# Attention block of a two-layer hybrid network: score products from stacked query halves, paired rms factors, and the first two query products placed ahead of the values

## The chip, the core and the metric

The kernel runs as one program on one core of a Trainium2 chip. The metric is the device time of one execution in microseconds. Five engines work side by side, each through its own instructions in a fixed order: TensorE (PE, with its weight loads shown as PEld), VectorE (DVE), ScalarE (ACT), GpSimd (POOL) and SyncE (SP). An instruction waits on semaphores for what it needs, and whatever is behind it on the same engine waits with it.

## The reference

The network has two layers, each a mixer and a feed-forward block with a short convolution. Layer 0 mixes by a convolution and a recurrence, layer 1 by sliding-window attention with a sink. Only the attention is touched here. T is 512, the width 1024, with 16 query heads in 4 groups that share 4 key and value heads of 64:

```python
h = rms_norm(x, norm_g)
qkv = h @ w_qkv + b_qkv
q = partial_rope(rms_norm(q, q_norm_g), positions)   # 16 heads
k = partial_rope(rms_norm(k, k_norm_g), positions)   # 4 heads
# blocks of 128 queries against the block before and their own: 256 keys
s = einsum('bnqhgd,bnkhd->bnhgqk', q, kc) * HEAD_DIM ** -0.5
s = where(valid, s, -inf)
m = maximum(max(s), sink)
pr = exp(s - m);  pr = pr / (sum(pr) + exp(sink - m))
o = einsum('bnhgqk,bnkhd->bnqhgd', pr, vc)
return o @ w_o + b_o
```

## The kernel before

Everything is kept transposed: a tile has 128 features in its partitions and the 512 positions along it. A large product goes as three products of halves: each weight chunk and each activation is split into a high half in the type fp32r and a low half, the rest. `gemm` (L162 to L175) loads a chunk of weights by SP (`wraw`, two buffers), makes its high half on ACT (`whi`, L150) and its low half on DVE (`wlo`, L151), with three buffers each, and issues twelve 128x512 matmuls (L174) for each half chunk of a single output block. A cast to `whi` can only start when PE is through with the half chunk three before it.

`attention` makes, in this order of the source: the products of the four key heads (two tiles), the row factor `rstd` (L224), the keys' own rms factor and rotation (`kr`) and their copy into the tiles `kd`, which hold a key head twice, in partitions 0 to 63 and again in 64 to 127; the values `vt` (L876, matmuls with 128x256); and then the queries, two heads a tile, by `queries(j)` for j = 0 to 7. `queries` reads its product out of PSUM (`zt`, L890), squares it on ACT (L892), sums the squares per position by sixteen tiny matmuls (L897), makes the rms factor `rq` of the two heads by five small DVE and two small ACT instructions (L902 to L910), and rotates the query (`rope`: four POOL DMAs into `zr`, then L836 to L838).

`block(m, b)` does the 4 heads of group m for the 128 queries of block b: four score matmuls in full fp32 (L931) from the 64 partitions of one head, each two instructions on the chip; on DVE the mask, the factor and the minimum (L936); the exponential on ACT (L101); the normaliser (L941 to L946, DVE); transposes on PE (L950) that ACT copies out (`pT`, L952); the product with the values (L957); and its split into `oh`, `ol` (L183 on ACT, L184 on DVE). The scores take the three PSUM banks of ring "c", two for each block.

The loop runs m from 0 to 3 and b from 0 to 3 in each, with `queries(2m+2)` and `queries(2m+3)` in between; `queries(0)` and `queries(1)` stand ahead of it. Then comes the output product with `w_o` (L174 again, 192 matmuls, 36 of which need only the first three groups). The order of the instructions on each engine is not that of the source: a scheduler, working from its own estimates, writes one fixed order per engine, and the chip keeps to it.

Of the kernel before, what the change touches and what calls it, by code (L numbers as in the profile page):

```python
# [11 lines left out]
F32 = mybir.dt.float32  # L12
F32R = mybir.dt.float32r
I32 = mybir.dt.int32
AF = mybir.ActivationFunctionType
ALU = mybir.AluOpType
# [3 lines left out]
P = 128  # L20
T = 512
D = 1024
DC = D // P
NB = T // P
# [11 lines left out]
NH = 16  # L36
NKV = 4
HD = 64
# [7 lines left out]
T3 = 5  # L46
# [22 lines left out]
class Net:  # L69
# [734 lines left out]
    def attention(self):  # L804
        nc, tc, ap = self.nc, self.tc, self.ap
        V, S, G = nc.vector, nc.scalar, nc.gpsimd
        wq, wo = ap["w_qkv"], ap["w_o"]
# [4 lines left out]
        xh, xl = self.xg_tiles()  # L812
        for m in range(DC):
            self.xg_chunk(xh, xl, "attn_norm_g", 0, m)
        with ExitStack() as es:
            pool = lambda **k: es.enter_context(tc.tile_pool(**k))
            cst = pool(name="atb", bufs=1)
# [7 lines left out]
            def rope(dst, z, j=None):  # L825
                t = tq("rp")
# [14 lines left out]
            kd = [cst.tile([P, T], F32, name=f"kd{m}") for m in range(NKV)]  # L841
# [11 lines left out]
            for i in range(2):  # L853
# [9 lines left out]
                kr = tq("kr")  # L863
                rope(kr, t)
                for e in range(2):
                    for o in range(2):
                        G.dma_start(kd[2 * i + e][o * HD : (o + 1) * HD, :], kr[e * HD : (e + 1) * HD, :])
# [15 lines left out]

            qr = cst.tile([P, 8, T], F32, name="qr")
            rq = cst.tile([P, NB, NH], F32, name="rq")

            def queries(j):
                pq = self.gemm(wq, j, xh, xl, m=1, pss=[self.bank("a")])[0]
                t = tq("zt")
                V.tensor_tensor(out=t, in0=pq, in1=rstd, op=ALU.mult)  # L890
                sq = tq("zs")
                S.activation(out=sq, in_=t, func=AF.Square, bias=self.pc("attn_b_qkv", j))  # L892
                pss = self.bank("d")[:, 0:8].rearrange("p (b h) -> p b h", b=NB)

                for b in range(NB):
                    for i in range(0, P, 32):
                        nc.tensor.matmul(pss[i : i + 32, b, :], lhsT=sq[:, b * P + i : b * P + i + 32], rhs=self.bh, start=True, stop=True,  # L897
                                         tile_position=(0, i))
                S.activation(out=t, in_=t, func=AF.Identity, scale=self.pc("attn_q_norm_g"), bias=self.bg[:, j : j + 1])

                ms = tr.tile([P, NB, 2], F32, tag="ms", name="ms")
                V.tensor_scalar(out=ms, in0=pss, scalar1=1.0 / HD, scalar2=1e-6, op0=ALU.mult, op1=ALU.add)  # L902
                rope(qr[:, j, :], t, j)
                y0 = tr.tile([P, NB, 2], F32, tag="my", name="my")
                self.fn(out=y0, in_=ms, func=AF.Ln)
                self.fn(out=y0, in_=y0, func=AF.Exp, scale=-0.5)
                V.tensor_tensor(out=ms, in0=ms, in1=y0, op=ALU.mult)
                V.tensor_tensor(out=ms, in0=ms, in1=y0, op=ALU.mult)
                V.tensor_scalar(out=ms, in0=ms, scalar1=0.5 / 8, scalar2=-1.5 / 8, op0=ALU.mult, op1=ALU.add)
                V.tensor_tensor(out=rq[:, :, 2 * j : 2 * j + 2], in0=ms, in1=y0, op=ALU.mult)  # L910

            cst.tile([P, 112], F32, name="gap")
# [3 lines left out]
            def block(m, b):  # L916
# [10 lines left out]
                for hp in range(2):  # L927
                    for e in range(2):
                        h = 4 * m + 2 * hp + e
                        hs = slice(e * HD, (e + 1) * HD)  # L930
                        nc.tensor.matmul(pscs[e][:, hp, :nk], lhsT=qr[hs, h // 2, bs], rhs=kd[m][hs, k0 : k0 + nk], start=True, stop=True)  # L931
# [29 lines left out]
            queries(0)  # L961
            queries(1)
# [82 lines left out]
```

## Time and profile before

| | us |
|---|---|
| median of three runs | 1217.86 (1217.53 to 1218.5) |
| the profiled execution | 1216.95 |
| its span in the trace | 1215.2 |
| PE busy, of the span | 1194.8 (98%) |
| DVE busy | 723.4 (60%) |
| ACT busy | 554.3 (46%) |

The time around the span is 1.75 us. The attention lies between about 668 and 850 us. In this document the block phase is the stretch from the first L936 (719.70 us) to the end of the last L946 (812.04 us). In a timeline row the first number is the start and the second the duration; PE durations are modelled and overlap, so what a matmul costs is read from the distance of two starts. In the table of windows each engine has its busy time and the count of its instructions.

### The profile page before, as it was taken

To read this page: it belongs to the slowest core of one execution; us is meant where nothing else is said; L and a number is where in the kernel's file an instruction comes from. 1 tells how busy PE (TensorE), PEld (TensorE's weight loads), DVE (VectorE), ACT (ScalarE), POOL (GpSimd) and SP (SyncE) were. 2 spreads that over 40 slices of the span, in tenths; PEclk is the share of its full clock that TensorE was granted. 3 is DMA by queue.
4 is the path that set the end of the run, shared out by engine and by line. 5 is a ranking of instruction groups with operands and counts; after the bars stand their busy time and mean duration, and the time that the engine had idled before them with its cause. 6 is when DMAs were issued, how large, how long until landed. Compare 5 with 4: busy or idle time off the path is not lost.

```text
span 1215.2 us, 16956 instructions
## 1 busy us (share of the span) xinstructions
PE 1194.8 (98%) x6419; PEld 940.5 (77%) x6419; DVE 723.4 (60%) x1366; ACT 554.3 (46%) x1035; POOL 72.0 (6%) x209
## 2 busy tenths in 40 slices
PE   6999999999999999999999999999999999999998
PEld 5777866568788888888888866668888888888886
DVE  6787866477766555553333778875555555553332
ACT  6878332374534444342222567764543343442221
POOL 4101031000100000000000031100000000000000
PEclk9999998999999999999999999999999999999999
DMA  6144291023322223233333231112222223233331
GB/s 191 37 130 113 96 221 38 2 88 103 97 92 104 94 97 104 87 104 96 96 96 95 87 95 57 41 36 90 101 90 101 103 89 104 88 103 112 113 113 61
DMA packets 65088, 114.43 MB, mean 94 GB/s; under 512 B 15680, under 2 KB 17936, under 8 KB 65008
## 3 DMA queue, kind: packets, MB, share of 16 engines
q1 hardware_dynamic: 60048, 102.25, 26.3%
q0 software_dynamic: 4816, 10.89, 3.5%
q8 instruction: 50, 0.82, 0.3%
q14 instruction: 30, 0.25, 0.1%
q10 hardware_dynamic: 144, 0.23, 0.1%
HBM read 105.40 MB, written 4.26 MB: 90 GB/s over the span
## 4 chain that ended last, share of the span: by engine, by line
PE 94%; DVE 2%; ACT 2%; DMA 1%; issue 1%; SPq 0%; DVEq 0%
PE mm L174 68%; PE bank L174 11%; PE mm L633 2%; PE bank L931 2%; PE bank L957 1%; PE bank L950 1%; PE ps L411 1%; PE ps L543 1%; DMA xT<-in_xT_dram 1%; PE ps L562 1%; PE ps L556 1%; PE ps L570 0%; PE bank L359 0%; PE ps L549 0%; PE ps L520 0%
## 5 line engine op out<-in xcount | busy, mean ns | idle before, releaser
L151 DVE TENSOR_TENSOR wlo<-wraw,whi 128x512 fp32r<-128x512 f32 x364 | 250.8, 690 | 348.0 <-ACT whi L150 347.4
L150 ACT CAST whi<-wraw 128x512 fp32r<-128x512 f32 x364 | 224.9, 619 | 421.3 <-PE mm L174 378.4
L174 PE MATMUL mm<-xgh,whi 128*128 128x512 f32 x896 | 350.9, 392 | 9.8 <-ACT whi L150 8.3
L174 PE MATMUL mm<-xgh,wlo 128*128 128x512 f32 x896 | 351.0, 392 | 0.2 <-DVE wlo L151 0.2
L174 PE MATMUL mm<-xgl,whi 128*128 128x512 f32 x896 | 350.5, 391 | 0.0
L174 PEld LDWEIGHTS mm<-xgh,whi 128*128 128x128 f32 x896 | 168.6, 188 | 47.0 <-ACT whi L150 10.1
L174 PEld LDWEIGHTS mm<-xgh,wlo 128*128 128x128 f32 x896 | 168.5, 188 | 38.7 <-issue 2.4
L174 PEld LDWEIGHTS mm<-xgl,whi 128*128 128x128 f32 x896 | 168.7, 188 | 35.8 <-issue 1.2
L174 PE MATMUL mm<-hh,whi 128*128 128x512 f32 x352 | 136.9, 389 | 0.0
L174 PE MATMUL mm<-hl,whi 128*128 128x512 f32 x352 | 136.9, 389 | 0.0
L174 PE MATMUL mm<-hh,wlo 128*128 128x512 f32 x352 | 136.9, 389 | 0.0
L174 PEld LDWEIGHTS mm<-hh,wlo 128*128 128x128 f32 x352 | 66.1, 188 | 13.8
L174 PEld LDWEIGHTS mm<-hh,whi 128*128 128x128 f32 x352 | 66.1, 188 | 13.8
L174 PEld LDWEIGHTS mm<-hl,whi 128*128 128x128 f32 x352 | 66.1, 188 | 13.5
L720 DVE SCALAR_TENSOR_TENSOR t<-gp,col,t 128x512 f32<-128x512 f32 x88 | 63.5, 745 | 0.0
L717 ACT ACTIVATE t<-gp,col 128x512 f32<-128x512 f32 x44 | 35.7, 816 | 35.3 <-DVE gp L715 34.7
L183 ACT CAST hh<-t 128x512 fp32r<-128x512 f32 x44 | 27.2, 622 | 36.8 <-DVE t L723 36.5
L715 DVE TENSOR_TENSOR gp<-mm,rstd 128x512 f32<-128x512 f32 x44 | 30.3, 692 | 17.3 <-PE mm L174 17.2
L723 DVE TENSOR_TENSOR t<-t,mm 128x512 f32<-128x512 f32 x44 | 30.1, 687 | 17.0 <-PE mm L174 17.0
L101 ACT ACTIVATE t<-t 128x512 f32<-128x512 f32 x44 | 27.7, 630 | 20.4 <-DVE t L720 20.3
L714 POOL MEMSET gp<- 128x2 f32 x44 | 4.5, 104 | 507.7 <-DVE t L720 451.0
L936 DVE CUSTOM_DVE_ANT_0 pr<-bank,mask,nsnk 128x256 f32<-128x256 f32 (+1 forms) x64 | 31.4, 503 | 1.9 <-PE bank L931 1.9
(328 smaller groups left out, 1433.6 us busy)
## 6 DMA issues: line engine op xcount, KB each, us to landing
wraw<-in_w_up_dram SPq DMA_DIRECT2D x88, 512.0 KB, 3.5
wraw<-in_w_down_dram SPq DMA_DIRECT2D x40, 512.0 KB, 3.5
wraw<-in_w_in_dram SPq DMA_DIRECT2D x22, 512.0 KB, 3.6
wraw<-in_w_qkv_dram SPq DMA_DIRECT2D x12, 512.0 KB, 3.5
wraw<-in_w_out_dram SPq DMA_DIRECT2D x8, 512.0 KB, 3.5
wraw<-in_w_o_dram SPq DMA_DIRECT2D x8, 512.0 KB, 3.5
st<-cpad POOLq DMA_DIRECT2D x24, 135.0 KB, 4.4
xT<-in_xT_dram SPq DMA_DIRECT2D x4, 512.0 KB, 8.2
```

The costliest lines, as they stand in the source:

```text
L101: ins = self.nc.scalar.activation(**kw)
L150: nc.scalar.copy(hi, src)
L151: nc.vector.tensor_tensor(out=lo, in0=src, in1=hi.bitcast(F32), op=ALU.subtract)
L174: mm = lambda a, b, **kw: self.nc.tensor.matmul(ps, lhsT=a[:, i, k, :], rhs=b[:, kk, :], **kw)
L183: nc.scalar.copy(hi, src)
L633: nc.tensor.matmul(pc[b * 32 : b * 32 + 32, :], lhsT=dg[:, b, g, :], rhs=stk[b][:, 4 * g : 4 * g + T], start=g == 0, stop=g == 7, tile_pos ...
L715: V.tensor_tensor(out=gp[:, 2:], in0=pg[i], in1=rstd, op=ALU.mult)
L717: S.activation(out=t, in_=gp[:, 2:], func=AF.Identity, scale=self.pc("ffn_conv_w", (3 * l + 2) * FC + f), bias=self.pc("ffn_conv_b", l * F ...
L720: V.scalar_tensor_tensor(out=t, in0=gp[:, j : j + T], scalar=self.pc("ffn_conv_w", (3 * l + j) * FC + f), in1=t, op0=ALU.mult, op1=ALU.add)
L723: V.tensor_tensor(out=t, in0=t, in1=pu[i], op=ALU.mult)
L931: nc.tensor.matmul(pscs[e][:, hp, :nk], lhsT=qr[hs, h // 2, bs], rhs=kd[m][hs, k0 : k0 + nk], start=True, stop=True)
L936: V.tensor_tensor_reduce(out=pr_[:, i, :nk], in0=pscs[e][:, hp, :nk], in1=mask[:, 2 * P - nk :], op0=ALU.add, op1=ALU.min, scale=rq[:, b, ...
```

## The change

The keys are split once into high and low fp32r halves (`ks`), and `kd` keeps both halves of a head, each in both partition halves. Each query tile is split after its rotation into `qh` (ACT) and `ql` (DVE), and four SP DMAs of 128 KB put them into `qs`, where a head has its high half in 64 partitions and its low half in the other 64. A score is now two fp32r matmuls over all 128 partitions, one with the keys' high and one with their low half, always over 256 keys (before: 128 in block b = 0). The rms factors are made for two query tiles at once: their sums of squares share one PSUM bank, and the small instructions run once for both. `queries(0)` and `queries(1)` now stand ahead of the values. The rotation's scratch `rp` and the tile `qr` moved to the ring "t2", and `kr` too.

```diff
-            kd = [cst.tile([P, T], F32, name=f"kd{m}") for m in range(NKV)]
+            kd = [cst.tile([P, 2, T], F32R, name=f"kd{m}") for m in range(NKV)]
+            pair = lambda n: tr.tile([P, 2, 2, T], F32R, tag="qs", name=n, bufs=2)
+            ks = pair("ks")
...
-                kr = tq("kr")
+                kr = t2("kr")
                 rope(kr, t)
+                self.split(ks[:, i, 0, :], ks[:, i, 1, :], kr)
                 for e in range(2):
                     for o in range(2):
-                        G.dma_start(kd[2 * i + e][o * HD : (o + 1) * HD, :], kr[e * HD : (e + 1) * HD, :])
+                        G.dma_start(kd[2 * i + e][o * HD : (o + 1) * HD].bitcast(F32), ks[e * HD : (e + 1) * HD, i].bitcast(F32))
...
             def queries(j):
...
-                pss = self.bank("d")[:, 0:8].rearrange("p (b h) -> p b h", b=NB)
+                if j % 2 == 0:
+                    qs["ps"] = self.bank("d")[:, 0:16].rearrange("p (b i h) -> p b i h", b=NB, i=2)
+                pss = qs["ps"][:, :, j % 2]
...
-                rope(qr[:, j, :], t, j)
+                qr = t2("qr")
+                rope(qr, t, j)
+                if j % 2 == 0:
+                    qs[j // 2] = pair("qs")
+                q = [tr.tile([P, T], F32R, tag="t2", name=n, bufs=T3) for n in ("qh", "ql")]
+                self.split(q[0], q[1], qr)
+                for e in range(2):
+                    for d in range(2):
+                        nc.sync.dma_start(qs[j // 2][d * HD : (d + 1) * HD, j % 2, e, :].bitcast(F32), q[d ^ e][e * HD : (e + 1) * HD, :].bitcast(F32))
+                if j % 2:
+                    ms = tr.tile([P, NB, 4], F32, tag="ms", name="ms")
...
+            queries(0)
+            queries(1)
             vt = cst.tile([P, NB, KD], F32, name="vt")
...
                 for hp in range(2):
-                    for e in range(2):
-                        h = 4 * m + 2 * hp + e
-                        hs = slice(e * HD, (e + 1) * HD)
-                        nc.tensor.matmul(pscs[e][:, hp, :nk], lhsT=qr[hs, h // 2, bs], rhs=kd[m][hs, k0 : k0 + nk], start=True, stop=True)
+                    for j in range(2):
+                        for e in range(2):
+                            nc.tensor.matmul(pscs[e][:, hp, :], lhsT=qs[m][:, hp, e, bs], rhs=kd[m][:, j, k0 : k0 + 2 * P], start=j == 0, stop=j == 1)
...
-            queries(0)
-            queries(1)
             for m in range(NKV):
```

The lines shift: the score matmul L931 becomes L948, L936 becomes L953, the values' L876 becomes L923, the sums of squares L897 become L888, and the transposes L950 become L967.

The scheduler's order changes with it. On PE 73 of the 192 query matmuls stand ahead of the first score matmul before, and 102 now. The two places below are those where the block phase begins.

On DVE before, up to the first instruction of the first block (`pr_6121`); `zt_6079` belongs to the third query tile, `ms` and `rq` are the rms factor's small instructions:

```order
L151 TENSOR_TENSOR wlo_6220<-wraw_6201,whi_6219 128x512
L836 TENSOR_TENSOR rp_5955<-zr0_5582,sgs_3292 128x512
L838 TENSOR_TENSOR qr_5891<-qr_5891,rp_5955 128x512
L890 TENSOR_TENSOR zt_6079<-bank_6044,rstd_5661 128x512
L151 TENSOR_TENSOR wlo_6368<-wraw_6365,whi_6367 128x512
L836 TENSOR_TENSOR rp_6029<-zr1_5583,sgs_3292 128x512
L902 TENSOR_SCALAR ms_6101<-bank_6083 128x8
L838 TENSOR_TENSOR qr_5891<-qr_5891,rp_6029 128x512
L837 TENSOR_TENSOR qr_5891<-zt_6079,cos_3252 128x512
L907 TENSOR_TENSOR ms_6101<-ms_6101,my_6111 128x8
L936 ISA pr_6121,nm_6119<-bank_6122,mask_3300,nsnk_3298,rq_5892 128x128
```

On DVE now, up to the same instruction (`pr_6136`); `ql_5914` is the low half of the second query tile, `wlo_6588` the weights' second half of the sixth, and `zt_6093` the third query tile:

```order
L184 TENSOR_TENSOR ql_5914<-qr_5904,qh_5913 128x512
L904 TENSOR_SCALAR ms_6296<-bank_6097 128x16
L908 TENSOR_TENSOR ms_6296<-ms_6296,my_6298 128x16
L909 TENSOR_TENSOR ms_6296<-ms_6296,my_6298 128x16
L910 TENSOR_SCALAR ms_6296<-ms_6296 128x16
L911 TENSOR_TENSOR rq_5772<-ms_6296,my_6298 128x4x4
L151 TENSOR_TENSOR wlo_6588<-wraw_6569,whi_6587 128x512
L836 TENSOR_TENSOR rp_6116<-zr0_5582,sgs_3292 128x512
L837 TENSOR_TENSOR qr_6115<-zt_6093,cos_3252 128x512
L838 TENSOR_TENSOR qr_6115<-qr_6115,rp_6116 128x512
L953 ISA pr_6136,nm_6134<-bank_6137,mask_3300,nsnk_3298,rq_5772 128x128
```

The factors of the third and fourth query tiles, a low half of the sixth tile's weights and the whole rotation of the third tile have come ahead of the first block.

On ACT before, up to the first exponential:

```order
L899 ACTIVATE zt_6005<-zt_6005,bg_3312,col_86 128x512
L101 ACTIVATE my_6037<-ms_6027 128x8
L101 ACTIVATE my_6037<-my_6037 128x8
L150 CAST whi_6219<-wraw_6201 128x512
L150 CAST whi_6367<-wraw_6365 128x512
L892 ACTIVATE zs_6081<-zt_6079,col_86 128x512
L899 ACTIVATE zt_6079<-zt_6079,bg_3312,col_86 128x512
L101 ACTIVATE my_6111<-ms_6101 128x8
L101 ACTIVATE my_6111<-my_6111 128x8
L101 ACTIVATE pr_6121,dn_6120<-pr_6121,nm_6119 128x128
```

On ACT now, from the high half of the first query tile (`qh_5840`) to the first exponential; `whi_6422` belongs to the fifth query tile's weights, `whi_6571` and `whi_6587` to the sixth's, `whi_6751` to the seventh's:

```order
L150 CAST whi_6422<-wraw_6404 128x512
L183 CAST qh_5840<-qr_5830 128x512
L881 ACTIVATE zs_6095<-zt_6093,col_86 128x512
L890 ACTIVATE zt_6093<-zt_6093,bg_3312,col_86 128x512
L150 CAST whi_6571<-wraw_6569 128x512
L183 CAST qh_5913<-qr_5904 128x512
L881 ACTIVATE zs_6260<-zt_6258,col_86 128x512
L890 ACTIVATE zt_6258<-zt_6258,bg_3312,col_86 128x512
L150 CAST whi_6587<-wraw_6569 128x512
L150 CAST whi_6751<-wraw_6749 128x512
L183 CAST qh_6125<-qr_6115 128x512
L101 ACTIVATE pr_6136,dn_6135<-pr_6136,nm_6134 128x128 x2
```

The splits of the queries stand behind weight casts, and each of those waits for PE to be through with the half chunk three before it.

## Rows read from the trace of the kernel before

**Rows 1.** Page, busy time, share of the span, instructions.

```profile
PE 1194.8 (98%) x6419; PEld 940.5 (77%) x6419; DVE 723.4 (60%) x1366; ACT 554.3 (46%) x1035; POOL 72.0 (6%) x209
```

**Rows 2.** Windows: stretch, length, then PE, PEld, DVE, ACT, POOL busy (instructions), clock, DMA.

```profile
684.80:719.70 34.90, 34.54 (x296) 26.67 (x295) 25.52 (x51) 17.80 (x33) 9.98 (x20) 1.00 0.40 111
719.70:812.04 92.34, 91.37 (x632) 57.94 (x631) 78.37 (x316) 69.57 (x218) 10.35 (x21) 1.00 0.13 39
812.04:814.68 2.64, 2.40 (x19) 1.35 (x18) 1.12 (x3) 1.74 (x4) 0.00 (x0) 1.00 0.03 6
```

**Rows 3.** Waits of DVE in the block phase: total us, times, longest.

```profile
DVE ol L184 <- ACT oh L183: 4.9, 11, 0.8
DVE ms L902 <- PE bank L897: 2.2, 4, 0.7
DVE pr L936 <- PE bank L931: 1.9, 5, 0.4
DVE zt L890 <- PE bank L174: 1.7, 3, 0.8
DVE dn L943 <- ACT nm L101: 1.5, 3, 1.0
DVE nm L941 <- ACT pr L101: 1.2, 2, 0.8
```

**Rows 4.** Timeline of DVE: rstd, around the first L936, the last L946.

```profile
684.80 0.43 DVE L224 COPY rstd<-rms_y 128x512 f32<-128x512 f32 x1
...
704.52 0.68 DVE L151 TENSOR_TENSOR wlo<-wraw,whi 128x512 fp32r<-128x512 f32 x1
705.12 0.68 DVE L838 TENSOR_TENSOR kr<-kr,rp 128x512 f32<-128x512 f32 x1
...
719.70 0.41 DVE L936 CUSTOM_DVE_ANT_0 pr<-bank,mask,nsnk 128x128 f32<-128x128 f32 x1 [0.36 <-PE bank L931]
...
810.90 1.14 DVE L946 TENSOR_SCALAR pr<-pr,dn 128x256 f32<-128x256 f32 x4
```

**Rows 5.** Timeline of PE: values' matmuls, query matmuls, the first scores, the end.

```profile
681.22 0.28 PE L876 MATMUL mm<-wlo,xgh 128*128 128x256 f32 x1
681.34 0.28 PE L876 MATMUL mm<-whi,xgl 128*128 128x256 f32 x1
...
698.02 0.39 PE L174 MATMUL bank<-xgl,whi 128*128 128x512 f32 x1
698.25 0.40 PE L174 MATMUL bank<-xgh,wlo 128*128 128x512 f32 x1
...
715.49 0.92 PE L931 MATMUL bank<-kd,qr 64*128 64x128 f32 x6
...
814.68 0.50 PE L174 MATMUL bank<-oh,whi 128*128 128x512 f32 x1
```

**Rows 6.** Windows of the score line alone: stretch, length, PE and PEld busy, clock, DMA.

```profile
719.70:812.04 92.34, 25.11 (x118) 14.16 (x116) 1.00 0.13 39
```

**Rows 7.** Timeline of PE: two runs of score matmuls and the matmul after each.

```profile
745.43 1.13 PE L931 MATMUL bank<-kd,qr 64*128 64x256 f32 x4
746.48 0.50 PE L174 MATMUL bank<-xgl,whi 128*128 128x512 f32 x1
...
783.38 1.56 PE L931 MATMUL bank<-kd,qr 64*128 64x256 f32 x8
784.87 0.50 PE L174 MATMUL bank<-oh,whi 128*128 128x512 f32 x1
```

**Rows 8.** Groups by form, 668 to 848 us: busy us, mean ns, idle before.

```profile
L902 DVE TENSOR_SCALAR ms<-bank 128x8 f32<-128x8 f32 x8 | 1.3, 164 | 2.9 <-PE bank L897 2.9
L150 ACT CAST whi<-wraw 128x512 fp32r<-128x512 f32 x40 | 24.7, 617 | 29.7 <-PE bank L174 23.1 <-PE mm L174 4.2 <-PE mm L876 2.3
L101 ACT ACTIVATE my<-my 128x8 f32<-128x8 f32 x8 | 1.7, 208 | 0.2
```

**Rows 9.** Tile kd: its DMAs from SBUF to SBUF, 128 KB each.

```profile
DMA to landing us min/median/max: 2.2/2.8/5.3
```

More of the change, by code (lines that the diff above doesn't have):

```diff
@@ L825, in rope @@
             def rope(dst, z, j=None):
-                t = tq("rp")
+                t = t2("rp")
                 if j is None:
@@ L838, in rope @@
                 V.tensor_tensor(out=dst, in0=dst, in1=t, op=ALU.add)
-            kd = [cst.tile([P, T], F32, name=f"kd{m}") for m in range(NKV)]
+            cst.tile([P, 56], F32, name="gap0")
+            kd = [cst.tile([P, 2, T], F32R, name=f"kd{m}") for m in range(NKV)]
+            pair = lambda n: tr.tile([P, 2, 2, T], F32R, tag="qs", name=n, bufs=2)
+            ks = pair("ks")
             pk = self.gemm(wq, 8, xh, xl)
@@ new lines, in attention, with queries @@
+            qs = {}
+            rq = cst.tile([P, NB, NH], F32, name="rq")
+            def queries(j):
+                pq = self.gemm(wq, j, xh, xl, m=1, pss=[self.bank("a")])[0]
+                t = tq("zt")
+                V.tensor_tensor(out=t, in0=pq, in1=rstd, op=ALU.mult)
+                sq = tq("zs")
+                S.activation(out=sq, in_=t, func=AF.Square, bias=self.pc("attn_b_qkv", j))
+                if j % 2 == 0:
+                    qs["ps"] = self.bank("d")[:, 0:16].rearrange("p (b i h) -> p b i h", b=NB, i=2)
+                pss = qs["ps"][:, :, j % 2]
+                for b in range(NB):
+                    for i in range(0, P, 32):
+                        nc.tensor.matmul(pss[i : i + 32, b, :], lhsT=sq[:, b * P + i : b * P + i + 32], rhs=self.bh, start=True, stop=True,
+                                         tile_position=(0, i))
+                S.activation(out=t, in_=t, func=AF.Identity, scale=self.pc("attn_q_norm_g"), bias=self.bg[:, j : j + 1])
+                qr = t2("qr")
[9 more added lines that the diff above has]
+                    ms = tr.tile([P, NB, 4], F32, tag="ms", name="ms")
+                    V.tensor_scalar(out=ms, in0=qs["ps"].rearrange("p b i h -> p b (i h)"), scalar1=1.0 / HD, scalar2=1e-6, op0=ALU.mult, op1=ALU.add)
+                    y0 = tr.tile([P, NB, 4], F32, tag="my", name="my")
+                    self.fn(out=y0, in_=ms, func=AF.Ln)
+                    self.fn(out=y0, in_=y0, func=AF.Exp, scale=-0.5)
+                    V.tensor_tensor(out=ms, in0=ms, in1=y0, op=ALU.mult)
+                    V.tensor_tensor(out=ms, in0=ms, in1=y0, op=ALU.mult)
+                    V.tensor_scalar(out=ms, in0=ms, scalar1=0.5 / 8, scalar2=-1.5 / 8, op0=ALU.mult, op1=ALU.add)
+                    V.tensor_tensor(out=rq[:, :, 2 * j - 2 : 2 * j + 2], in0=ms, in1=y0, op=ALU.mult)
@@ L881, in attention @@
                 V.scalar_tensor_tensor(out=vt[:, b, :], in0=pvs[b][:, :KD], scalar=rt[:, b : b + 1], in1=self.bvr, op0=ALU.mult, op1=ALU.add)
[L884 to L892, printed above, removed]
-                pss = self.bank("d")[:, 0:8].rearrange("p (b h) -> p b h", b=NB)
[L895 to L902, printed above, removed]
-                rope(qr[:, j, :], t, j)
[L904 to L912, printed above, removed]
+            cst.tile([P, 56], F32, name="gap")
             oh = cst.tile([P, DC, T], F32R, name="oh")
```

## Prediction

> **What bounds the kernel now.** The page comes first: PE is busy for 98% of the span, DVE for 60% [rows 1]. That says "PE" for the whole kernel; it need not hold for the stretch that the change touches. So the attention is cut into windows next [rows 2]: from the row factor (684.80 us) to the first block, the block phase (719.70 to 812.04), and the tail until PE takes up the last 156 matmuls of the output product, which run without a break. In the block phase PE is busy for 91.4 of 92.3 us, but DVE for 78.4 and ACT for 69.6. The waits of DVE there [rows 3] name 13.4 of its 14.0 idle us: 7.6 behind ACT (4.9, 1.5, 1.2), which are latencies inside a block, and only 5.8 behind PE (2.2, 1.9, 1.7). So the phase has two near-bounds. Taking work from PE alone can win about those 5.8 us; after that DVE's own work, its order and its start set the end.
>
> The Trainium skill says the same in another way: "Perfetto Trace Analysis", section "Identifying the Most-Contended Engine", holds that the share of matmul busy time is a poor measure for TensorE and wants the busy share of the weight loads, and occupancy for VectorE. In the block phase that is 57.9 us of weight loads against 78.4 us of DVE [rows 2], so by that rule DVE is the contended engine there; by the matmul row PE is. By the first a lighter PE brings little, by the second it brings its whole price; this is what divides the forecast from the first rival.
>
> **PE: what the scores save.** 64 calls, 128 instructions on the chip, of which 118 lie in the phase with 25.1 us [rows 6], 0.21 us each. Afterwards there are 128 matmuls of 128x256 in fp32r; the values' matmuls have that form and follow each other at 0.12 us [rows 5]. Some 122 of them in the phase are 14.6 us: PE gets 10.5 us lighter. In block b = 0 the 256 columns instead of 128 are included. The bounds are from the runs [rows 7]: four instructions take 1.05 us to the next start, eight take 1.49, so the second four cost 0.44, 0.11 each, no more than a full-row matmul. What is dear is the head of a run; the saving is between 0 (no heads) and 10.5 us, and I take 10.5 since the 25.1 is a sum over all runs.
>
> The Trainium skill speaks against the change here: "TensorEngine Tiling (Array Packing)", section "Theoretical Speedup", gives two products with a contraction of at most 64 up to twice the rate when they sit in different row tiles. The two heads of a pair already do, and the 0.11 us agrees; by that rule alone stacking saves next to nothing, and by the sum over the runs 10.5 us. The forecast below hardly depends on it.
>
> **PE: what moves out of the phase.** 102 query matmuls instead of 73 stand ahead of the first score: 29 more at 0.23 us [rows 5] are 6.7 us that leave the phase and go in front of it. PE's phase work falls from 91.4 to about 74 us, below DVE's. The sums of squares and values' matmuls keep their number.
>
> **The start of the block phase.** This is where I see the loss. From 684.8 to the first score (715.49) PE is busy for nearly all of the time [rows 2, 5], so 6.7 us more of its work delay that score by 6.7 us. Two things come on top.
>
> First, one of the four value banks is the bank of the second query tile's product, and the sums of squares of that tile wait for the same reading. DVE has this reading behind the whole chain of the second key tile (L202, L203, L865, L830, L837, L838), where before it was the first query that stood there. PE has from 681.2 us on [rows 5] 48 query matmuls (11.1 us), 54 value matmuls (6.5) and some 2.9 us of small products until it is there, at 701.7; DVE ended that chain at 705.80 before [rows 4] and I put it about a microsecond earlier now, as the vector work of the values is no longer within it. The wait is between 0 and 3 us; I take 1.7.
>
> Second, the first L953 stands behind the sixth tile's weights (`wlo_6588`) and three rotation instructions. The cast for it waits until PE is through the first half of the fifth tile's product: six query matmuls, six scores and sixteen small sums after the first score, about 2.5 us; then ACT 0.62 [rows 8], DVE 0.60 and 1.9 for the rotation (a 128x512 instruction each 0.60 [rows 4]): 5.5 us from first score to first L953, where it was 4.2 (715.49 to 719.70): +1.3. The query halves travel in this time: cast, subtraction and a DMA of 2.2 to 2.8 us [rows 9]; they land at about the time PE comes to them, so I count 0, and up to 2 if they take the 5.3 of the slowest.
>
> The start is late by 6.7 + 1.7 + 1.3 = 9.7 us, bounds 6.7 and 12.
>
> **DVE's work in the phase.** By the order, between first L936 and last split, these go: 18 small rms instructions (of 0.16 us [rows 8], half hidden beside others: 1.8), three weight halves (1.8), one reading of a query product (0.6), two rotation instructions (1.2); six query low halves come (3.6). Sum -2.0, from 78.4 to about 76.4 us; bounds -3 and -1. The two halves of the keys and two of the queries fall ahead of the phase and are in the start.
>
> **DVE's idle time in the phase.** The 7.6 us behind ACT stay: the order within a block is the same. The 5.8 behind PE mostly go, but one new wait takes their place: the seventh query tile has 13 of its 24 matmuls in one run behind the last values' product of group 1, and DVE must read that tile before it begins group 2. From the end of a last L946 to the end of the values' product it is 2.64 us [rows 2]; with 13 matmuls at 0.23 that is 5.6, less about 1.6 of DVE work in between: 4.0. Idle is 11.6 instead of 14.0: -2.4, bounds 5 and 16 us idle, -9 and +2.
>
> **At nothing:** ten more casts on ACT (6.2 us) less eight pairs of small ones made in four (1.7, [rows 8]), since ACT has 22.8 us idle in the phase; if that cover goes, it is the exponentials behind a weight cast that are late, in the bounds of the idle time. The 32 new SP DMAs stand between weight loads on SP's queue, with DMA engines 13% busy [rows 2]; the weights have two buffers of lead, cost 0, up to 2 us if a load comes late behind a query half. The keys' eight DMAs on POOL carry twice the bytes and have over 10 us until their use. Behind the phase nothing changes: 156 output matmuls, then the second feed-forward block.
>
> **The sum.** +9.7 - 2.0 - 2.4 = +5.3 us on the profiled execution's 1216.95: 1222.3. The median of the runs shown is 0.9 higher, so 1223.2. The check: the new phase would have 92.3 - 9.7 = 82.6 us to break even, DVE needs 76.4, so its idle time would have to fall from 14.0 to 6.2 us, less than the waits behind ACT alone.
>
> **Rivals.**
> 1. PE is the bound and stays it. Then the 6.7 us only change places and the scores' 10.5 us come off, less the 1.7 of the wait: -8.8, 1209. For it: 91.4 of 92.3 us; against it: DVE's 78.4 us in the same stretch. Chance 0.15.
> 2. No change that can be seen. The start is late by the 6.7 us alone, DVE loses the waits behind PE without the new one: 6.7 - 2.0 - 5.8 = -1.1, 1217. Chance 0.16. This needs the reading of the second query to be early and the halves to be on time.
> 3. Heavier: with ACT's splits behind weight casts and those behind PE, the engines wait in a ring, and idle time goes to 16 us with the start at its later bound: 12 - 2 + 2 = +12, 1230. Chance 0.12. It decides once PE's run of query matmuls and DVE's need of their splits fall apart by more than a weight half chunk (2.8 us).
> The forecast has 0.57.
>
> **Chances and range.** About 0.2%, 2.4 us, is what a measurement of this kernel tells from no change. Slower: 0.57 and 0.12 less a little for the forecast's low edge, 0.67. Same: 0.16. Faster: rival 1 and the low edge of rival 2, 0.17. The forecast's own range goes from the low start with idle time down by 9 (6.7 + 1.3 - 3 - 9 = -4.0, 1214) to +12 (1230); that holds rivals 2 and 3. Rival 1 lies outside; I let the low end reach a microsecond further towards it, to 1213.
>
> **What would show it.** Right: the first L953 at about 729 us on the old scale, DVE busier than before in the phase and PE with some 10 us or more of idle time in it, the last L963 later than 812 by about 5 us, a wait of PE in the values' matmuls behind L879, and a wait of DVE for a query product after group 1. Wrong: a first L953 before 726, DVE idle time under 7 us, or PE still without idle time in the phase.

## The result, and the profile after

The changed kernel takes 1232.4 us (median of 1229.3 to 1233.8), the kernel before beside it 1218.2: a ratio of 1.011, 95% interval 1.0087 to 1.0134, 14 us slower. The prediction was 1223.2, slower by 5.3, with a range of 1213 to 1230. The profiled execution, the slowest of the four shown, has a span of 1232.1 us, 16.9 more than before.

The busy line of the page first [rows 1], then the same three windows as in [rows 2]: from the row factor to the first reading of scores (now L953), the block phase, the tail.

```profile
PE 1199.6 (97%) x6419; PEld 950.2 (77%) x6419; DVE 727.7 (59%) x1356; ACT 557.5 (45%) x1037; POOL 71.9 (6%) x209
```

```profile
688.88:737.41 48.53, 44.95 (x379) 36.46 (x378) 31.81 (x59) 22.82 (x40) 12.13 (x24) 0.96 0.53 146
737.41:827.00 89.59, 80.25 (x558) 54.63 (x556) 76.38 (x300) 66.94 (x212) 8.08 (x16) 0.94 0.24 64
827.00:831.53 4.53, 4.26 (x20) 2.16 (x20) 0.42 (x1) 1.76 (x4) 0.00 (x0) 0.62 0.28 105
```

The first window grew by 13.6 us (34.90 to 48.53). The block phase lost 2.8, though PE has 9.3 us idle in it instead of 1.0. The tail grew by 1.9, at a granted clock of 0.62 where it was 1.00. No line ahead of attention was touched; all the same it begins later, as its first row sum shows (PE's timeline, first of after, then of before):

```profile
683.80 1.05 PE L222 MATMUL ps<-sq,ones_d 128*128 128x512 f32 x2
```

```profile
680.22 1.04 PE L222 MATMUL ps<-sq,ones_d 128*128 128x512 f32 x2
```

From here on, "start" is counted from this L222 to the first reading of scores: 39.5 us before (680.22 to 719.70), 53.6 after. So the 16.9 us are +3.6 ahead of attention, +14.1 in the start, -2.8 in the phase, +1.9 behind it.

What the start waits for: VectorE's timeline of the changed kernel around the first query tile (start, duration, line, what it writes and reads, idle time before it).

```profile
721.45 1.30 DVE L151 TENSOR_TENSOR wlo<-wraw,whi 128x512 fp32r<-128x512 f32 x2 [3.54 <-ACT whi L150]
722.66 0.69 DVE L836 TENSOR_TENSOR rp<-zr,sgs 128x512 f32<-128x512 f32 x1
...
726.64 0.68 DVE L184 TENSOR_TENSOR ql<-qr,qh 128x512 fp32r<-128x512 f32 x1
...
735.47 0.69 DVE L836 TENSOR_TENSOR rp<-zr,sgs 128x512 f32<-128x512 f32 x1 [1.77 <-DMA zr<-zt]
...
737.41 0.41 DVE L953 CUSTOM_DVE_ANT_0 pr<-bank,mask,nsnk 128x128 f32<-128x128 f32 x1
```

The first rotation (L836) stands behind weight halves that wait for TensorE to give buffers back, then come the split (726.64) and the halves' transfer; the first score runs at 730.08. Then the reading stands behind the third tile's rotation, which waits 1.77 us for its DMA. In this start the rotation's 16 KB DMAs land in this many us (minimum, median, maximum), before and after:

```profile
DMA to landing us min/median/max: 1.7/2.6/5.0
```

```profile
DMA to landing us min/median/max: 2.2/5.0/7.9
```

VectorE's waits in the phase, where [rows 3] had 14.0 us in many short ones:

```profile
DVE ol L184 <- ACT oh L183: 5.6, 6, 2.9
DVE wlo L151 <- PE bank L174: 3.0, 1, 3.0
DVE zt L879 <- PE bank L174: 1.9, 2, 1.7
```

### The profile page after: what moved, and what is told of

Read it like the earlier page. It is cut to its first block, busy times and chain, and to the rows that moved or that the text cites. A ratio compares the mean times of both kernels' runs of the same rounds, so it can differ in the third digit from the quotient of the medians.

```text
span 1232.1 us, 17046 instructions
## 1 busy us (share of the span) xinstructions
PE 1199.6 (97%) x6419; PEld 950.2 (77%) x6419; DVE 727.7 (59%) x1356; ACT 557.5 (45%) x1037; POOL 71.9 (6%) x209
## 3 DMA queue, kind: packets, MB, share of 16 engines
q1 hardware_dynamic: 62608, 106.45, 27.9%
## 4 chain that ended last, share of the span: by engine, by line
PE 90%; ACT 4%; DVE 3%; DMA 1%; issue 1%; SPq 0%; POOL 0%; DVEq 0%; ACTq 0%
PE mm L174 67%; PE bank L174 10%; PE mm L633 2%; PE bank L967 1%; PE ps L411 1%; PE bank L974 1%; PE bank L948 1%; DMA xT<-in_xT_dram 1%; PE ps L562 1%; PE ps L543 1%; PE ps L556 1%; PE mm L923 1%; ACT pr L101 1%; ACT pT L969 1%; PE ps L570 0%
## 5 line engine op out<-in xcount | busy, mean ns | idle before, releaser
L174 PEld LDWEIGHTS mm<-hh,whi 128*128 128x128 f32 x352 | 66.1, 188 | 13.7
L174 PEld LDWEIGHTS mm<-hh,wlo 128*128 128x128 f32 x352 | 66.1, 188 | 13.6
L717 ACT ACTIVATE t<-gp,col 128x512 f32<-128x512 f32 x44 | 35.7, 816 | 35.3 <-DVE gp L715 34.7
L186 ACT ACTIVATE xgh<-xT,col 128x512 fp32r<-128x512 f32 x32 | 22.6, 718 | 20.4 <-DVE xT L987 8.1
```

Of the source, the lines that this page charges most:

```text
L174: mm = lambda a, b, **kw: self.nc.tensor.matmul(ps, lhsT=a[:, i, k, :], rhs=b[:, kk, :], **kw)
L186: nc.scalar.activation(out=hi, in_=src, func=AF.Identity, scale=scale)
L717: S.activation(out=t, in_=gp[:, 2:], func=AF.Identity, scale=self.pc("ffn_conv_w", (3 * l + 2) * FC + f), bias=self.pc("ffn_conv_b", l * F ...
```

## The experiments

Medians are of all runs of a kernel; the other times are from its profile, in us. "L222" is where attention's first row sum begins, "start" runs from there to the first reading of scores, and "phase" from there to the end of the last L946 (by its new number). "Behind" is from that to the end of the span. The ratio is to the kernel before, with its 95% interval.

| kernel | median | ratio | L222 | start | phase | behind |
|---|---|---|---|---|---|---|
| before | 1216.5 to 1218.2 | | 680.2 | 39.5 | 92.3 | 403.2 |
| changed | 1232.4 | 1.0087 to 1.0134 | 683.8 | 53.6 | 89.6 | 405.1 |
| changed, again (g4) | 1231.7 | 1.0105 to 1.0135 | 680.3 | 54.6 | 88.3 | 405.7 |
| late order (e1) | 1224.8 | 1.0045 to 1.0071 | 680.4 | 52.3 | 85.9 | 404.5 |
| order alone (e2) | 1218.7 | 0.9996 to 1.0015 | 680.5 | 37.8 | 93.2 | 404.5 |
| pairs alone (e3) | 1217.4 | 0.9990 to 1.0008 | 680.1 | 40.0 | 91.5 | 403.6 |
| stacking alone (e4) | 1225.5 | 1.0049 to 1.0081 | 681.8 | 52.2 | 86.7 | 403.1 |
| changed, priority (f1) | 1225.3 | 1.0039 to 1.0080 | 681.3 | 46.6 | 91.8 | 404.4 |
| changed, rotation by matmul (f2) | 1225.3 | 1.0043 to 1.0082 | 680.3 | 46.7 | 91.7 | 402.9 |
| late, rotation by matmul (f2 late) | 1220.3 | 1.0009 to 1.0033 | 679.5 | 46.4 | 88.4 | 404.0 |
| changed, 64 matmuls more (f4) | 1235.9 | 1.0129 to 1.0170 | 679.4 | 56.1 | 93.0 | 405.7 |
| f2 late, tiles behind blocks (g1) | 1233.4 | 1.0108 to 1.0140 | 681.6 | 45.3 | 101.8 | 402.7 |
| f2, tiles behind blocks (g2) | 1233.0 | 1.0113 to 1.0142 | 680.0 | 42.3 | 106.0 | 404.0 |
| before, rotation by matmul (g3) | 1224.9 | 1.0051 to 1.0080 | 681.3 | 38.1 | 100.8 | 404.2 |
| f2 late, first block first (h1) | 1219.8 | 1.0019 to 1.0042 | 679.7 | 44.7 | 90.1 | 402.7 |
| late, priority (h2) | 1225.1 | 1.0050 to 1.0078 | 680.0 | 50.2 | 89.2 | 404.3 |
| f2 late, low halves on GpSimd (h3) | 1219.5 | 1.0010 to 1.0030 | 680.1 | 45.0 | 89.9 | 402.7 |
| f2 late, two tiles by matmul (i1) | 1224.2 | 1.0040 to 1.0067 | 680.8 | 44.7 | 92.0 | 404.8 |
| h1, two tiles by matmul (i2) | 1224.5 | 1.0034 to 1.0076 | 680.9 | 45.7 | 90.8 | 404.8 |
| h3, two tiles by matmul (i3) | 1219.0 | 0.9998 to 1.0023 | 681.3 | 43.8 | 89.6 | 402.7 |

### Which part costs

Late order: the two calls go back behind the values. Order alone: the kernel before with them moved ahead. Pairs alone: the kernel before with the changed `ms` lines. Stacking alone: late order, with the `ms` lines of before.

```diff
-            queries(0)
-            queries(1)
             vt = cst.tile([P, NB, KD], F32, name="vt")
...
+            queries(0)
+            queries(1)
             for m in range(NKV):
```

> The changed kernel with the first two query tiles made behind the values again, as in the kernel before; stacked scores and paired rms factors stay. Theory O (the order is what costs: the 29 query matmuls and the waits around them stand ahead of the first score): the start of the block phase, from L222 of attention to the first reading of scores, comes back from 53.6 us to 42 to 44, and the time from 1232 to 1221 to 1223, a few us above before for the halves' transfers. Theory S (the splitting and the stacking cost, by the rotation's DMA that lands late behind the halves' transfers and by the lower clock of a TensorE with less to do): the start stays at 50 us or more and the time at 1228 to 1232.

> The kernel before with the first two query tiles made ahead of the values and nothing else changed. Theory O: the start of the block phase grows from 39.5 us to 48 to 50 and the time to 1226 to 1229. Theory S: the order alone costs at most 3 us, since the halves' transfers are absent: 1218 to 1221. A third theory (the first score no longer waits for the queries, but the values end as late as the same work takes in any order): within 2 us of before.

> The kernel before with the rms factors of the queries made for two tiles at once and nothing else changed: four groups of small VectorE operations fewer. By the pass that is on the path in the block phase it should gain 2 to 4 us (1214 to 1216). Rival: the factors of the first two tiles now wait for the second query tile, so the first reading of scores is no earlier, and the rest lies in VectorE's idle time: 1218, no change.

> The changed kernel with the order of before and the rms factors of before: of the change only the splitting and the stacked scores are left. Theory O: within 4 us of before (1218 to 1222), the start of the block phase at 42 to 44 us. Theory S: 1226 to 1231, a start of 48 us or more, and a granted clock under 0.9 in the block phase, where before had 1.00.

Pairs: nothing. Order alone: nothing that can be told from zero. Its first score even comes 28.0 us after L222 instead of 35.3, with 48 query matmuls ahead of it instead of 73, since a score needs no value; the first reading, only 1.7 us earlier, the phase (+0.9) and what lies behind it (+1.3) take that back. PE's first scores in that run:

```profile
708.55 0.92 PE L934 MATMUL bank<-kd,qr 64*128 64x128 f32 x6
```

Theory O falls. Stacking alone: +8 us, with the whole late start, 52.2 us, in the old order. That is theory S for the start; the times of the two late runs are below its ranges (1224.8 and 1225.5), and the granted clock of the phase in stacking alone is 0.96, not under 0.9. Stacking alone also carries the move of `rp`, `qr` and `kr` to the ring "t2", which no run takes by itself. The first rotation of the kernel before, and then VectorE's timeline of stacking alone:

```profile
713.91 0.69 DVE L836 TENSOR_TENSOR rp<-zr,sgs 128x512 f32<-128x512 f32 x1 [0.16 <-DMA zr<-zt]
```

```profile
719.84 0.69 DVE L151 TENSOR_TENSOR wlo<-wraw,whi 128x512 fp32r<-128x512 f32 x1 [2.03 <-ACT whi L150]
720.45 0.69 DVE L836 TENSOR_TENSOR rp<-zr,sgs 128x512 f32<-128x512 f32 x1
...
723.58 0.69 DVE L184 TENSOR_TENSOR ql<-qr,qh 128x512 fp32r<-128x512 f32 x1
```

and PE's first score there:

```profile
728.18 0.47 PE L940 MATMUL bank<-kd,qs 128*128 128x256 f32 x2 [0.24 <-DMA zr<-zt]
```

(A score reads no `zr`; the row names what came last by the profile.) Counted from L222, the first rotation is at 38.7 us (before: 33.7) and the score 7.7 us behind it (before: 1.6): 5.0 + 6.1 = 11.1 us for the first score. Part of the 5.0 begins on POOL's queue. Rotation DMAs of the first query tile stand there around the keys' DMAs, and these now wait for the keys' split; the row names the small `rq` instruction right behind that split on VectorE (first before, then stacking alone):

```profile
706.51 2.11 POOL L867 DMA_DIRECT2D kd<-kr  x4
708.61 1.02 POOL L835 DMA_DIRECT2D zr<-zt  x2
```

```profile
710.11 2.08 POOL L871 DMA_DIRECT2D kd<-ks  x4 [1.97 <-DVE rq L899]
712.17 0.52 POOL L835 DMA_DIRECT2D zr<-zt  x1
```

The tile's last rotation DMA is issued 30.4 us after L222, 28.9 before. In stacking alone it is the one that takes longest of the rotation's DMAs in the start, 6.0 us:

```profile
DMA to landing us min/median/max: 2.3/4.1/6.0
```

So it lands at 718.2, 36.4 us after L222, where the rotation of before, which waits for this landing, begins at 33.7: 2.7 of the 5.0 us. The other 2.3 us the landed data wait on VectorE, behind a weight half that itself waited 2.03 us for its cast (the first row above). The 6.1 are an instruction of the rotation that now stands behind L836, two others ahead of the low half, the split and the halves' DMAs, whose median is 2.8 us there. TensorE is not idle meanwhile (50.5 of the 52.2 us): later query matmuls, planned for the phase, fill the time, and 113 of them stand ahead of the first score, in the old order. That is why the phase gets shorter, by 5.6 us, but not by the 12.7 that the start grew.

On the stacked kernel the early order then costs 7 us more (1224.8 to 1231.7 or 1232.4). Going by the profiles of e1 and of the changed kernel's second execution (span 1223.1 and 1228.9) it is +2.3 in the start, +2.4 in the phase and +1.2 behind; which wait causes it the runs do not single out.

### The chain to the first score

Priority: rotation, split and transfers are ranked 400 places earlier for the scheduler (in h2 for the first two tiles only). Rotation by matmul: the queries take the keys' way, product with the permutation, in place of four DMAs each.

```diff
+                with tc.high_priority(offset=400):
...
-                if j is None:
-                    pp = self.bank("d")
+                if True:
+                    pp = self.bank("d" if j is None else "b")
```

> The changed kernel in which the rotation, the split and the halves' transfers of each query tile are placed ahead of the weight casts that stand before them on VectorE (in the changed kernel the first rotation, L836, comes on VectorE behind five wlo of the values' weights, which wait 3.5 us and less for TensorE to give buffers back). Theory R (the place of the rotation and the split in VectorE's queue is what makes the first score late): first score 39 to 42 us after L222 of attention instead of 46.3, time 1225 to 1228. Theory D (the transfers themselves, rotation 4 us and halves 2.4 us behind keys on POOL's queue, make it late): first score 45 us or more after L222 and 1230 to 1233.

> The changed kernel with the queries rotated by the permutation matmul that the keys use, in place of the four zr DMAs of each query tile: no rotation waits on POOL's queue or for a landing. TensorE gets 8 fp32 rotations more, about 1 us each by the 2.3 us of the four records of two key tiles, in place of idle time. Theory D: first score at 38 to 41 us after L222 and 1222 to 1227. Theory R: VectorE's queue is what holds it, but without the landing the rotation is placed earlier too; the first score comes as early as in the run with priority, and the time is within 2 us of that run. Theory C (the lower clock of a waiting TensorE costs most): first score earlier, but the block phase no shorter and 1230 or more.

> Stacked scores, paired rms factors, the order of before (first two query tiles behind the values) and the queries rotated by the permutation matmul. By the measured 1224.8 of the late order with zr DMAs: theory D gives 5 to 8 us less, 1217 to 1220, as before or a little below; theory R gives 1219 to 1222; theory C gives 1223 to 1226, since the block phase keeps its waits.

> Stacked scores, paired factors, late order, rotation by the DMAs as in the change, and the rotation and split of the first two query tiles placed early on VectorE. The late order alone gave 1224.8 with a start of 52.3 us; the same edit of place on the changed kernel took 7 us off both. Theory R: start 45 to 47 us, 1217 to 1219. Theory D (the rotation's landings bind once VectorE does not): start 49 us or more, 1221 to 1224.

On the changed kernel either edit gives 7 us back in the start, 53.6 to 46.6, and 7 in the time. With priority that is theory R (first score 40.8 us after L222). With matmuls the first score is at 45.3, which no theory had, with the reading only 1.4 us behind it; the time fits D and R alike. With the late order, matmuls give 4.5 us (1220.3, in R's range and a little above D's) and priority nothing (1225.1; R had 1217 to 1219, D 1221 to 1224), though the first rotation now begins 31.4 us after L222, earlier than before the change. So with priority the two orders take the same time (f1 and h2, 1.0060 and 1.0064 of before); with matmuls the early one still costs 5 us. What holds the late run with priority is first of all a landing. PE's timeline of that run:

```profile
721.11 0.76 PE L946 MATMUL bank<-kd,qs 128*128 128x256 f32 x2 [3.68 <-DMA zr<-zt]
721.67 0.63 PE L174 MATMUL bank<-xgl,whi 128*128 128x512 f32 x1
722.10 0.63 PE L174 MATMUL bank<-xgh,wlo 128*128 128x512 f32 x1
...
729.27 0.39 PE L174 MATMUL bank<-xgl,whi 128*128 128x512 f32 x1
729.49 0.39 PE L174 MATMUL bank<-xgh,wlo 128*128 128x512 f32 x1
```

PE stands 3.68 us. The row names a rotation's DMA, but a score reads the halves: those were issued from 714.15 to 717.95 and took this long (minimum, median, maximum), so it is their landing, not the rotation's, that D should have named:

```profile
DMA to landing us min/median/max: 5.1/5.5/6.0
```

For some 5 us after the wait the matmuls follow at 0.43 us instead of 0.22, and the granted clock is 0.50 from 721.11 to 726.37: part of the wait is paid a second time at the lower clock. The reading then comes only 9.0 us behind the score, for VectorE stands there for a weight cast and for the third tile's product:

```profile
724.27 0.69 DVE L151 TENSOR_TENSOR wlo<-wraw,whi 128x512 fp32r<-128x512 f32 x1 [5.55 <-ACT whi L150]
...
728.55 0.69 DVE L879 TENSOR_TENSOR zt<-bank,rstd 128x512 f32<-128x512 f32 x1 [2.99 <-PE bank L174]
```

The Trainium skill, "DMA: Bandwidth & Descriptors", section "Anatomy of one DMA — SWDGE (gpsimd) path", puts a fixed 2.0 us on each transfer that GpSimd issues, beside a small part for its bytes. The rotation's 16 KB DMAs go that way: their fastest landing in the changed kernel's start, 2.2 us, agrees; their median there, 5.0, is not in that rule.

### Which engine bounds the phase

> The kernel before with the queries rotated by the permutation matmul and nothing else changed. If TensorE is the bound of the block phase before (idle 0.5 us of the 92), six tiles of 1.0 us (the two records of L829 end 1.0 us after the first begins) in the phase and two at its start add 6 to 8 us: 1223 to 1226. If VectorE is the bound, as the prediction had it: the matmuls lie beside its work, 1216 to 1219.

> The run that gave 1220.3 with the lower half of each query tile subtracted on GpSimd in place of VectorE (8 instructions of 0.69 us less on VectorE). Theory V (VectorE is the bound of the block phase once scores are stacked: 80.0 us busy of 88.4): the phase falls by 2 to 4 us, 1216 to 1218. Theory P (TensorE is still the bound, 84.4 us busy of 88.4 by the records): the phase stays within 1 us, 1219 to 1222; above that GpSimd's longer subtraction makes the halves late.

> The changed kernel with the first of the two score matmuls of each head issued twice (the first of the two writes nothing that is used): 64 matmuls of 0.118 us more, 7.6 us of TensorE work in the block phase, 4 a block. Theory C (the granted clock falls because TensorE idles, 0.70 in the window 767 to 782 us, and that costs 3 us or more): the clock stays at 1.00 there and the time falls or holds, 1228 to 1232. Theory W (waits for VectorE and the start cost, the clock little; TensorE has idle time for it): 1231 to 1234. Theory P (TensorE is again the bound in the phase): 7 us more, 1237 to 1240.

The first edit below is that of f4 (its start and stop flags follow), the second that of h3.

```diff
-                    for j in range(2):
+                    for j in (2, 0, 1):
...
-                self.split(q[0], q[1], qr)
+                S.copy(q[0], qr)
+                G.tensor_tensor(out=q[1], in0=qr, in1=q[0].bitcast(F32), op=ALU.subtract)
```

The kernel before with eight fp32 rotations on TensorE: +7.7 us, as expected of a TensorE that bounds the phase. Its two windows, start and phase:

```profile
681.33:719.38 38.05, 37.70 (x291) 29.56 (x290) 26.78 (x52) 18.97 (x34) 4.16 (x8) 1.00 0.37 108
719.38:820.20 100.82, 100.66 (x678) 62.12 (x676) 80.14 (x320) 70.41 (x221) 0.00 (x0) 1.00 0.10 34
```

PE is busy all the time, and the phase is 8.5 us longer, so TensorE had no room for the added matmuls. The rule of the Trainium skill that the prediction weighed ("Perfetto Trace Analysis", section "Identifying the Most-Contended Engine") judges how much room TensorE has by its FLOP rate and its weight loads, not by the busy time of its matmuls. By the weight loads (58 of 92 us before) VectorE was the contended engine of the phase. The measurement differs: the matmul row was the better witness here.

In the stacked kernel with the rotation by matmul, taking eight subtractions off VectorE leaves the time within the intervals (phase 88.4 to 89.9): theory V is not borne out. Theory P's time came, though the phase moved by 1.5 us, not within 1. And 64 score matmuls more in the changed kernel (their first writes are not used) cost about 4 us, between what theories W and P gave; the clock still fell, to 0.73 from 765.5 to 780.5 us, so this does not tell what the clock alone costs. It tells that the idle TensorE of the changed phase could take about half of 7.6 us of work for nothing.

### An early start alone does not pay

> Stacked scores, paired factors, late order and rotation by matmul as in the run that gave 1220.3, with two edits to the place of work alone: the rotation and split of the first two query tiles are placed early, and each later query tile is made behind the block it stood ahead of. In the run before, the first reading of scores (L950) stood on VectorE behind the rotation of the third query tile, which waited 5.3 us for its matmul (718.6 to 723.9), and TensorE stood 2.0 us for the halves' landing. Theory R (the place in VectorE's and TensorE's queues makes the start late): start 40 to 42 us instead of 46.4, and 1213 to 1217. Theory N (what the start gives back, the block phase takes, since VectorE's work there only moves): 1219 to 1222, with a block phase 3 us longer.

> The changed kernel (queries ahead of the values) with the rotation by matmul and the same two edits of place. Theory R: the first score no longer waits for the third tile and for late halves, start 40 to 43 us instead of 53.6, time 1217 to 1220. Theory N: 1223 to 1226, as with the rotation by matmul alone (1225.3). Theory O (the early order itself still costs): 2 us or more above the late order with the same edits.

> As the run that gave 1220.3 (stacked scores, paired factors, late order, rotation by matmul), with the rotation and split of the first two query tiles placed early and the third query tile alone made behind the first block; the later tiles keep their places. Theory R (the late start is the whole cost of stacking; the tiles' lead over the blocks has to stay): start 40 to 43 us, phase 88 to 90, 1214 to 1217. Theory L (any query tile that is made later comes back in the block phase, as in the run where all later tiles moved, 101.8 us of phase): phase 94 us or more and 1221 to 1226.

```diff
-                    if m < NKV - 1 and b % 2 == 0:
-                        queries(2 * m + 2 + b // 2)
                     block(m, b)
+                    if m < NKV - 1 and b % 2 == 0:
+                        queries(2 * m + 2 + b // 2)
```

In the late run with matmuls the reading stood on VectorE behind the third tile's rotation:

```profile
717.92 0.68 DVE L151 TENSOR_TENSOR wlo<-wraw,whi 128x512 fp32r<-128x512 f32 x1
723.90 0.69 DVE L830 TENSOR_TENSOR rp<-bank,sin 128x512 f32<-128x512 f32 x1 [5.29 <-PE bank L829]
...
725.83 0.40 DVE L950 CUSTOM_DVE_ANT_0 pr<-bank,mask,nsnk 128x128 f32<-128x128 f32 x1
```

Making every later tile behind its block, with the first two ranked early, gave the start 1.1 us (late order) and 4.4 (early order), and cost the phase 13.5 and 14.3. In the late order the loss is spread over all four groups of heads: from one group's first reading to the next they take 28.0, 28.1 and 27.8 us and the last 17.9 to its end, where f2 late has 23.3, 26.1, 24.0 and 15.0. In the last stretch VectorE and PE are both far from full:

```profile
801.91:828.75 26.84, 21.18 (x107) 12.54 (x106) 17.76 (x71) 16.13 (x51) 0.00 (x0) 0.87 0.18 54
```

Both theories were too kind (expected 1213 to 1226, measured 1233). Theory O has nothing here: the two orders take the same time. With the third tile alone moved (and the first two ranked early), 1219.8: the start 1.6 earlier, the phase 1.7 longer, which is neither R (1214 to 1217) nor L (a phase of 94 or more). Theory R falls as the whole story: in these runs what the start gives back, the phase takes, and with all tiles moved it takes far more, so the lead of the query tiles over the blocks is worth more than an early first reading.

### Two tiles by matmul

> As the run that gave 1220.3 (stacked scores, paired factors, late order), but only the first two query tiles are rotated by matmul; the six later ones, which have a lead over their blocks, are rotated by the DMAs again. If the transfers cost only where the first score waits for them and TensorE is near its bound in the phase (85 us busy of 88), six rotations of 1.0 us go from TensorE's phase and the first reading of scores no longer stands behind the third tile's rotation: start 40 to 43 us, phase 84 to 88, 1212 to 1216, which would beat the kernel before. If the later tiles' chains bind in the phase too (transfers of rotation and halves one behind the other), the phase grows by 2 us or more: 1218 to 1224.

> The same with the first two tiles' rotation and split placed early and the third tile made behind the first block (1219.8 with all eight rotated by matmul). First theory: 1212 to 1216. Second: 1219 to 1224.

> The same as the first of these with the lower halves subtracted on GpSimd (1219.5 with all eight rotated by matmul), which shares its queue with the rotation's DMAs. First theory: 1212 to 1216. Second: the DMAs wait behind GpSimd's subtractions and the phase grows: 1219 to 1225.

```diff
-                if True:
+                if j is None or j < 2:
```

Six rotations of about a microsecond leave TensorE and the phase grows from 88.4 to 92.0 us. So the rotation's DMAs cost in the phase here, and not only ahead of it, as the second theory had it. With the subtraction on GpSimd there is no loss against all eight by matmul (1219.0 and 1219.5; phase 89.6 and 89.9); why is open, and with it what in the DMAs costs. No kernel tried beats the one before by more than its interval.

### The changed kernel again

> The changed kernel again, unaltered. In its profiled execution the untouched stretch ahead of attention was 3.6 us late (L222 of attention at 683.8; 679.4 to 681.8 in the profiles of all the others). If that belongs to one execution: L222 at 679 to 682 here, and a median of 1229 to 1231. If it belongs to the program: L222 at 683 to 685 again and 1232 to 1234.

L222 is at 680.3 in this profile, so the 3.6 us ahead of attention belong to that one execution (its clock was 0.74 from 195 to 210 us; 1.00 here and before). The median, 1231.7, is above the 1229 to 1231 that I wrote for that case, in which the profiled execution, the fastest of the four, lies; where the others lose more is not shown. This profile's 13.7 us over before are +0.1, +15.2 (start), -4.1 (phase), +2.5 (behind), and so nearer to the medians' 14.

## Why the prediction was wrong

The direction was right; the size was not, and the direction owes something to luck, as its main term had a wrong reason. The failed step is "the start of the block phase", +9.7 with bounds 6.7 and 12: it is +15.2 (14.1 in the first profile). The phase, at -4.1 in the second profile, is near the -4.4 of the sum; the start's 5.5 us and 2.5 behind the phase, put at nothing, make up the miss. Rival 3 did not foresee it either: its start was 12 at most, and VectorE's 16 us of idle time in the phase did not come.

- **Its reason was wrong.** The 6.7 us were the query matmuls ahead of the values; e2 makes that move alone and loses nothing. I read the later first score off the number of matmuls ahead of it, 102 instead of 73. But that number is 48 with the order alone (e2) and 113 with stacking in the old order (e4): it goes with how late the score's operands are, not with the place of the two calls.
- **What was costed at nothing is the cause.** The query halves "land at about the time PE comes to them, so I count 0", and the keys' DMAs on POOL "have over 10 us until their use". e4 has both and not the order: start +12.7. The rotation is 5.0 us late (2.7 by a DMA that is issued behind the keys' split and lands later, 2.3 on VectorE behind a weight half), split and halves stand behind the rotation (+6.1), and the next reading waits in line (+1.6). The changed kernel with the rotation ranked early (f1) bears out the place on VectorE: its first rotation begins 11 us earlier (27.9 us after L222 instead of 38.9) and its first score 5.5. The 5.3 us landing that I named as the slowest came up as 5.6 (halves) and 7.9 (rotation).
- **1.7 us of TensorE behind L879, 1.3 behind the weights.** The first came, 1.4 us. The second is 3.1 us (4.2 to 7.3), of which 1.8 are the wait for the third tile's rotation.
- **VectorE's work in the phase**, -2.0: 78.4 to 76.4, exact, with some luck: the listed terms add up to -1.8, and two weight halves (12 to 10) and one rotation instruction left it, not three and two. **Its idle time**, -2.4: 14.0 to 13.2, and 12.0 in the second profile. The wait behind the seventh tile's run, put at 4.0, is there: 3.0 us for a weight half and 1.7 for the product.
- **PE's saving, 10.5 us and worthless.** Neither half held. The score line is busy for 21.6 us in the phase instead of 25.1 [rows 6], 0.18 us each and not 0.12 (its clock was 0.94; in the runs with 1.00 it is 20.0 to 24.1):

```profile
737.41:827.00 89.59, 21.60 (x118) 0.94 0.24 64
```

  and a little TensorE work is worth its price before the change (g3). With the same rotation by matmul, stacked, paired scores gain 4.6 us (1224.9 to 1220.3): rival 1's mechanism is there, but in the change, with its transfers, the time does not fall.
- **Behind the phase**, 0: +1.9 and +2.5. PE is at the lower clock in the tail (0.62) after a phase with waits; eight transposes took 2.11 us at its end (granted clock 0.50) and 1.14 in the phase (1.00).

```profile
807.56 1.14 PE L967 MATMUL bank<-ident,pr 128*128 128x128 f32 x8 [0.76 <-DVE pr L963]
...
828.12 2.11 PE L967 MATMUL bank<-ident,pr 128*128 128x128 f32 x8
```

Of the signs I named, two came as said, the wait behind L879 and VectorE's behind the tile after group 1, and one nearly: PE is idle for 9.3 us in the phase. VectorE's share of it hardly moved (85% both times). The first reading is at 737.4, 733.8 on the old scale and not 729. The last L963 ends at 827.0, 15 us later and not 5 (3.6 of it from ahead of attention). None of the signs of being wrong came: those looked for less waiting, not more.

What stays open: what the lower clock alone costs, what the move to the ring "t2" does by itself, and through which waits the early order costs the stacked kernel 7 us that it does not cost the other.

## What to carry to other kernels

When an operand gets a split and a copy between its product and its first use, price that chain as latency, transfer by transfer, with landings from a crowded stretch and with what each queue already holds, before pricing work saved on the engine that uses it. A count of instructions ahead of a late one can be a symptom; ask what it waits for. And an engine that is 99% busy in a stretch should be tried with a microsecond of extra work before its savings are called worthless.

## What was not expected of the hardware

- Two waits of TensorE were followed by half speed. In h2, after 3.68 us idle, the granted clock was 0.50 (1.2 instead of 2.4 GHz) and matmuls came 0.43 us apart where they come 0.22 apart at 1.00, for about 5 us. In f2 late, after 2.03 us idle, it was 0.50 for about 3 us, from 719.57 to 722.54.
- A 16 KB copy within SBUF landed in 2.6 us (median) in the old start and in 5.0 in the new one, with the DMA share of the windows at 0.40 [rows 2] and 0.53.
- The order that costs nothing without stacking (interval -0.04 to +0.15%) costs 7 us with it: the parts of a change to a scheduled kernel do not add up.
